# Products with V over 128 + 128 + 80 keys per 64 queries, in a windowed attention and convolution block

## The chip, the cores and the metric

The kernel runs on one core of a Trainium2 chip. The metric is device time in microseconds, from runs of the whole program; the profile is one execution, recorded by the hardware profiler. Short names: PE is TensorE's matmul stream and PEld its weight loads, DVE is VectorE, ACT ScalarE, POOL GpSimd, SP SyncE, which here only issues DMAs.

## What is computed

One encoder layer over two sequences (256 and 2048 tokens, so 2 + 16 blocks of 128) with 16 learned meta tokens ahead of each: RMSNorm, one input projection, a windowed attention group beside a convolution group, gates, one output projection, and the residual. What matters here is the attention of a real query t: it sees all 16 meta keys and the real keys s with |t - s| <= 128, in 8 heads of 64 with 2 key/value heads.

```python
kw = concatenate([kp[:, :-2], kp[:, 1:-1], kp[:, 2:]], axis=2)   # left, own and right block
vw = concatenate([vp[:, :-2], vp[:, 1:-1], vp[:, 2:]], axis=2)
s_win = einsum('bnqkgd,bnskd->bnkgqs', qb, kw) * scale - slopes * dist   # -inf outside the window
s_meta = einsum('bnqkgd,bmkd->bnkgqm', qb, km) * scale
p = softmax(concatenate([sink_b, s_meta, s_win], axis=-1), axis=-1)
o = einsum('bnkgqm,bmkd->bnqkgd', p[..., 1:17], vm) + einsum('bnkgqs,bnskd->bnqkgd', p[..., 17:], vw)
```

Outside the sequence there are no keys: blocks 0 and 2 have no left neighbour, blocks 1 and 17 no right one. These four are called edge blocks here, the other fourteen full blocks.

## The kernel before

Matrix operands are kept as a high and a low part in a 32-bit format (float32r), so that a product takes two or three matmuls. The first two thirds of the time are the input projection (`proj_et`, `proj_te`, lines 830 to 861) with the convolution on DVE; then come attention and the output projection.

Attention goes by steps of eight slots (`slot_step`, line 599). Step s computes the scores of block s and, for block s - 1, the products with V; the output projection (`outproj`, line 575) gives two pieces of three 512-column matmuls to every slot. The first 14 slots run between projection groups (`spread`, line 632), the rest in `attention_rest` (line 653). In that last stretch the order of the work on PE and on POOL is the program's own (`MAN2`); the orders of DVE, ACT and SP come from a planner's simulated times. `tick` ends a slot, and `later(k, f)` puts f off by k ticks.

- **Scores** (`scores`, line 376): each slot takes 32 queries of the 4 heads of one key/value head, as 128 rows, in two matmuls into one PSUM bank. A full block's window is `SW` = 304 keys wide (128 + 16 meta + 128 + 32). DVE adds the position bias and takes the minimum (`bias_max`, line 403), ACT does the exponential (`expo`), and after the fourth slot of a head group `norm` (line 427) divides on POOL; it first writes the 16 meta columns out to a tile `pm` (line 430).
- **Transposes** (`bank`, line 455): `plan` (line 448) lists them: for each key/value head and each tile of 128 keys (left, own, right) four 128x128 transposes of the probabilities, which load the probabilities as weights and stream the identity. Between the two heads stands one meta bank of two transposes, of `pm`. ACT copies the high part, DVE subtracts for the low part (`split`, line 464).
- **Products** (`pv_mm`, line 492): two matmuls of 512 columns for each tile of keys and head, high and low part. The meta product (`pv_meta`, line 499) is one further matmul of 512 columns for each head; its operand is spread over the heads by two masked products on POOL (`spread_meta`, line 480), and its weights `vm` hold the meta V eight times (eight DMAs, line 1135).
- **Loads** (on SP): `load_k` (line 281) issues one or two DMAs for a block into one of two key tiles, at slot 0 of the step before its use; `load_v` (line 289) one DMA of 128 KB for a block, in five buffers.

`merge` (line 517) adds the halves of the product and gates it on POOL with `gat`, which `load_ga` loads at slot 1.

Of the kernel before, what the change touches and what calls it, by code (L numbers as in the profile page):

```python
# [18 lines left out]
P = 128  # L19
# [60 lines left out]
def hymba_kernel(  # L80
# [29 lines left out]
    vec = const.tile([P, 30], F32, name="vec")  # L110
# [4 lines left out]
    snk, msk, nsnk = vec[:, 22:24], vec[:, 24:28], vec[:, 28:30]  # L115
    vm = const.tile([P, KV, P], F32R, name="vm")
# [114 lines left out]
    vt, qt, q2t, sbt, pmt, gat, gct, cnt, mix, att, yot, opj = ({} for _ in range(12))  # L231
# [3 lines left out]
    def attention_open():  # L235

        phase[0] = 2
        right_pools.close()
        man = ExitStack()
        cst['man'] = man  # L240
        man.enter_context(tc.manual_schedule(engines=MAN1))
        ap = att_pools.enter_context(tc.tile_pool(name="ap", bufs=2, side="right", reuse_waits="tile"))
        pool["a"] = ap
        cst["bias"] = bias = ap.tile([P, KV, 4, SW], BF16, tag="bias", name="bias", bufs=1)
        load_q(0)
        for i in range(2):
            kw.append(ap.tile([P, 2, KV, 400], F32R, tag=f"kw{i}", name=f"kw{i}", bufs=1))
        load_k(0)
        nc.sync.dma_start(bias, bias_c)
        for t in kw:  # L250
            nc.gpsimd.tensor_copy(t[:, :, :, P : P + NM], km)
        for i in range(3):
            t = ap.tile([P, 4, 400], F32, tag=f"sb{i}", name=f"sb{i}", bufs=1)
            for n in range(4):
                if n > 0:
                    nc.vector.memset(t[:, n, 0 : QB * n], 0.0)
                if n < 3:
                    nc.vector.memset(t[:, n, QB * n + SW : 400], 0.0)
            sbs.append(t)
        load_v(0)  # L260
        load_v(1)
# [17 lines left out]
    vt, qt, q2t, sbt, pmt, gat, gct, cnt, mix, att, yot, opj = ({} for _ in range(12))  # L279

    def load_k(b):
        if has_left(b):
            nc.sync.dma_start(kw[b % 2][:, :, :, 0:P].bitcast(F32), kd[:, :, :, P * (b - 1) : P * b])
        hi = P * (b + 2) if has_right(b) else P * (b + 1)
        nc.sync.dma_start(
            kw[b % 2][:, :, :, P + NM : P + NM + hi - P * b].bitcast(F32), kd[:, :, :, P * b : hi]
        )
# [88 lines left out]
    def scores(b, kv, n):  # L376

        c0 = QB * n if has_left(b) else P
        c1 = QB * n + SW if has_right(b) else min(QB * n + SW, 400 - P)
        w = c1 - c0  # L380
        if n == 0:
            sbt[b, kv] = sbs[(2 * b + kv) % 3]
            stat[b, kv] = (
                pool["a"].tile([P, 4], F32, tag="nm", name=f"nm{b}_{kv}", bufs=3),
                pool["a"].tile([P, 4], F32, tag="rs", name=f"rs{b}_{kv}", bufs=3),
                pool["a"].tile([P, 4], F32, tag="es", name=f"es{b}_{kv}", bufs=3),
            )
            if kv == 0:
                pmt[b] = pool["a"].tile([P, KV, 2, 4, NM], F32, tag="pm", name=f"pm{b}", bufs=1)
# [37 lines left out]
        def norm():  # L427
            nc.vector.tensor_tensor(es, es, rs, op=ALU.add)
            nc.vector.reciprocal(es, es)
            nc.gpsimd.tensor_tensor(  # L430
                pmt[b][:, kv],
                sb[:, :, P : P + NM].unsqueeze(1).to_broadcast([P, 2, 4, NM]),
                es.unsqueeze(1).unsqueeze(3).to_broadcast([P, 2, 4, NM]),
                op=ALU.mult,
            )
            for k in range(4):
                a0 = QB * k if has_left(b) else P
                a1 = QB * k + SW if has_right(b) else min(QB * k + SW, 400 - P)
# [9 lines left out]
    def plan(b):  # L448
        ks = ([0] if has_left(b) else []) + [1] + ([2] if has_right(b) else [])
        return [(k, 0) for k in ks] + [("m", 0)] + [(k, 1) for k in ks]  # L450

    KCOL = (0, P + NM, 2 * P + NM)
    pv_st = {}

    def bank(b, k, kv):
        pt = psum.tile([P, 4, P], F32, tag="b", name=f"pT{b}_{k}_{kv}")
        if k == "m":
            for i in range(KV):
                nc.tensor.transpose(pt[:, i, :], pmt[b][:, i].rearrange("p a h m -> p (a h m)"), ident)  # L459
        else:  # L460
            for hl in range(4):
                nc.tensor.transpose(pt[:, hl, :], sbt[b, kv][:, hl, KCOL[k] : KCOL[k] + P], ident)  # L462

        def split():
            if k == "m":
                ph = pool["a"].tile([P, KV, P], F32R, tag="phm", name=f"phm{b}", bufs=1)
                nc.scalar.copy(ph, pt[:, 0:KV, :])
                nc.vector.tensor_tensor(ph[64:128], pt[64:128, 0:KV, :], ph[64:128], op=ALU.subtract)
                later(1, lambda: spread_meta(b, ph))
                return  # L470
            ph, pl = (pt_part(2 * (n_bank[0] % 3) + i) for i in range(2))
            n_bank[0] += 1
            nc.scalar.copy(ph, pt)  # L473
            nc.vector.tensor_tensor(pl, pt, ph, op=ALU.subtract)  # L474
            pv_st[b, k, kv] = (ph, pl)

        later(1, split)
        later(3 if k == "m" else 2, lambda: pv(b, k, kv))

    def spread_meta(b, ph):  # L480

        pd = cst["pt"][:, 6:8].rearrange("p a (j n) -> p a j n", n=P)
        for kv in range(KV):
            nc.gpsimd.tensor_tensor(
                pd[:, kv],
                ph[:, kv : kv + 1, :].to_broadcast([P, 4, P]),
                msk.unsqueeze(2).to_broadcast([P, 4, P]),
                op=ALU.mult,
            )
        pv_st[b, "m"] = pd  # L490

    def pv_mm(b, kv, lhs, hs, start, stop):
        if start:
            opj[b, kv] = psum.tile([P, 4, P], F32, tag="c", name=f"O{b}_{kv}")
        o = opj[b, kv]
        for i, t in enumerate(hs):
            nc.tensor.matmul(o, lhs, t, start=(start and i == 0), stop=(stop and i == 1))  # L497

    def pv_meta(b, kv, stop):
        pin(stop)(nc.tensor.matmul)(  # L500
            opj[b, kv], vm[:, kv, :], pv_st[b, "m"][:, kv], start=False, stop=stop
        )

    def pv(b, k, kv):
        if k == "m":
            pv_meta(b, 0, True)
            later(1, lambda: merge(b, 0))
            return
        ks = [x for x, y in plan(b) if y == kv and x != "m"]
        first, last = k == ks[0], kv == 1 and k == ks[-1]  # L510
        pv_mm(b, kv, vt[b - 1 + k][:, kv, :], pv_st[b, k, kv], first, last)
        if kv == 1 and first:
            pv_meta(b, 1, False)
        if last:
            later(1, lambda: merge(b, 1))
# [83 lines left out]
    def slot_step(s_, slot):  # L599
        a, bb = s_, s_ - 1  # L600
        has_a, has_b = a < NB, 0 <= bb < NB
        steps = plan(bb) if has_b else []
        if slot == 0:
# [11 lines left out]
        if slot < len(steps):  # L615
# [59 lines left out]
    if True:  # L675
# [424 lines left out]
        nc.sync.dma_start(vec[:, 0:28], vecs)  # L1100
# [130 lines left out]
def layout(inputs):  # L1231
# [58 lines left out]
```

## Time and profile before

| | |
|---|---|
| time, median of 3 runs | 955.31 us (954.71 to 955.47) |
| span of the profiled execution | 953.4 us |
| instructions | 16429 |
| matmuls and transposes on PE | 5813 |
| busy share PE / PEld / DVE / ACT / POOL | 99% / 94% / 79% / 45% / 35% |
| moved by DMA | 170.88 MB, mean 179 GB/s |

For the profiled execution only its span is given, from the first to the last instruction; the time of a run also holds what lies around it. A busy PE is not PE at its peak: the ends of matmuls are modelled and overlap the next one's start, so distances between starts, and the pieces of the chain of waits, are the measure of what an instruction costs.

### The profile page before, as it was taken

What the parts mean: (1) busy time and instruction counts of PE and PEld (TensorE: products, weight loads), DVE (VectorE), ACT (ScalarE), POOL (GpSimd) and SP (SyncE); (2) the same over time, 40 slices, a digit from 0 to 9 for tenths busy, and PEclk for the clock granted to TensorE, in tenths of its full rate; (3) what the DMA queues carried; (4) which work ended last, traced back from release to release, by engine and by line L of the source; (5) the groups of instructions that cost most, each with busy time, mean ns of one, the idle gap of its engine ahead of it and who ended that gap; (6) DMA issues with size and microseconds to landing.
All of it is one profiled execution on the core that took longest, in us unless ns stands there. A gap on an engine that the chain in (4) does not pass through costs nothing.

```text
span 953.4 us, 16429 instructions
## 1 busy us (share of the span) xinstructions
PE 948.1 (99%) x5813; PEld 893.4 (94%) x5813; DVE 756.9 (79%) x1282; ACT 427.4 (45%) x1170; POOL 336.6 (35%) x518
## 2 busy tenths in 40 slices
PE   9999999999999999999999999999999999999998
PEld 8999999999999999999999999988888888888887
DVE  5579999997977879999995666677776777767773
ACT  7432022353458750011112446666665666656661
POOL 3320000282488300000001446556454544545442
PEclk9999999999999999999999999999999999999999
DMA  8575345785656594233333587945554455544311
GB/s 296 174 262 202 133 174 182 252 294 175 185 179 193 194 319 145 89 113 138 131 138 133 175 289 271 383 148 179 169 167 128 144 162 163 167 129 142 130 56 67
DMA packets 121585, 170.88 MB, mean 179 GB/s; under 512 B 9984, under 2 KB 84112, under 8 KB 121504
## 3 DMA queue, kind: packets, MB, share of 16 engines
q1 hardware_dynamic: 121504, 169.84, 53.3%
q8 instruction: 46, 0.75, 0.3%
q14 instruction: 35, 0.29, 0.1%
HBM read 107.10 MB, written 62.70 MB: 178 GB/s over the span
## 4 chain that ended last, share of the span: by engine, by line
PE 92%; DVE 3%; DMA 3%; SPq 1%; issue 1%; POOL 0%; ACT 0%; DVEq 0%; POOLq 0%; ACTq 0%
PE pj L837 42%; PE y L583 20%; PE pj L853 12%; PE O L497 5%; PE pT L462 4%; PE S L349 4%; PE O L349 1%; DVE y L920 1%; PE lnu L220 1%; PE lnt L201 1%; PE qT L349 1%; DMA wraw<-in_w_in 1%; DMA kd<-ks 1%; DMA vmd<-vs-1_2072 1%; PE pT_m L459 0%
## 5 line engine op out<-in xcount | busy, mean ns | idle before, releaser
L837 PE MATMUL pj<-xh,ws 128*128 128x384 f32 (+1 forms) x1536 | 395.9, 338 | 0.1
L920 DVE SCALAR_TENSOR_TENSOR y<-us,cw,y 128x1167 f32<-128x1167 f32 x240 | 328.7, 1422 | 0.4
L837 PEld LDWEIGHTS pj<-xh,ws 128*128 128x128 f32 x1536 | 280.0, 188 | 0.4 <-ACT xh L1090 0.4
L837 PE MATMUL pj<-xl,ws 128*128 128x384 f32 (+1 forms) x768 | 260.9, 340 | 0.1
L583 PE MATMUL y<-wo,rest 128*128 128x512 f32 (+1 forms) x672 | 173.7, 396 | 0.0
L853 PE MATMUL pj<-ws,xh 128*128 128x256 f32 (+1 forms) x880 | 165.6, 284 | 0.4 <-DVE qs L984 0.3
L837 PEld LDWEIGHTS pj<-xl,ws 128*128 128x128 f32 x768 | 144.1, 188 | 0.5 <-DVE xl L775 0.4
L853 PEld LDWEIGHTS pj<-ws,xh 128*128 128x128 f32 (+1 forms) x880 | 136.4, 187 | 1.4 <-issue 0.5
L583 PEld LDWEIGHTS y<-wo,rest 128*128 128x128 f32 x672 | 116.5, 189 | 19.6
L853 PE MATMUL pj<-ws,xl 128*128 128x256 f32 (+1 forms) x440 | 123.9, 282 | 0.0
L416 ACT ACTIVATE sb<-sb,nm 128x304 f32<-128x304 f32 (+4 forms) x144 | 77.1, 536 | 64.8 <-DVE nm L404 62.7
L945 ACT ACTIVATE go<-pj 128x384 f32<-128x384 f32 x48 | 23.6, 491 | 155.7 <-PE pj L837 141.6
L474 DVE TENSOR_TENSOR ptiles<-pT,ptiles 128x512 fp32r<-128x512 f32 x100 | 68.5, 685 | 30.6 <-ACT ptiles L473 29.8
L404 DVE CUSTOM_DVE_ANT_0 sb<-S,bias,vec 128x304 f32<-128x304 f32 (+4 forms) x144 | 73.6, 511 | 17.0 <-PE S L349 14.4
L128 POOL TENSOR_SCALAR ssk<-ssk 128x2 f32<-128x2 f32 x18 | 7.5, 419 | 213.4 <-ACT sqk L959 211.4
L853 PEld LDWEIGHTS pj<-ws,xl 128*128 128x128 f32 (+1 forms) x440 | 82.2, 187 | 0.3
L439 POOL TENSOR_SCALAR sb<-sb,es 128x304 f32<-128x304 f32 (+4 forms) x144 | 72.3, 519 | 3.5
L473 ACT CAST ptiles<-pT 128x512 fp32r<-128x512 f32 x100 | 58.0, 580 | 32.3 <-PE pT L462 31.5
L497 PE MATMUL O<-ptiles,v 128*128 128x512 f32 x200 | 64.8, 402 | 0.0
L349 PEld LDWEIGHTS S<-kw,q 128*128 128x128 f32 x288 | 53.2, 188 | 11.0
L349 PE MATMUL S<-kw,q 128*128 128x304 f32 (+4 forms) x288 | 62.1, 297 | 0.0
L128 POOL TENSOR_SCALAR ssq<-ssq 128x4 f32<-128x4 f32 (+2 forms) x55 | 30.3, 550 | 87.4 <-ACT xn L700 69.7
(127 smaller groups left out, 1277.0 us busy)
## 6 DMA issues: line engine op xcount, KB each, us to landing
wd<-ws SPq DMA_DIRECT2D x36, 512.0 KB, 6.0
ws<-wd SPq DMA_DIRECT2D x36, 512.0 KB, 5.9
wraw<-in_w_in SPq DMA_DIRECT2D x52, 256.0 KB, 6.0
xn<-in_z SPq DMA_DIRECT2D x18, 512.0 KB, 5.3
gd<-go SPq DMA_DIRECT2D x48, 192.0 KB, 2.0
yo<-in_z SPq DMA_DIRECT2D x36, 256.0 KB, 3.3
out_y<-yo SPq DMA_DIRECT2D x35, 256.0 KB, 2.2
kw<-kd SPq DMA_DIRECT2D x16, 512.0 KB, 5.0
```

Of the source, the lines that this page charges most:

```text
L349: r = f(*a, **k)
L404: nc.vector.tensor_tensor_reduce(out=sb[:, n, c0:c1], in0=ps[:, 0:w], in1=cst["bias"][:, kv, n, c0 - QB * n : c1 - QB * n], scale=1.0, sca ...
L416: nc.scalar.activation(sb[:, n, c0:c1], sb[:, n, c0:c1], AF.Exp, bias=nm[:, n : n + 1], scale=-1.0, accum_out=rs[:, n : n + 1],)
L439: nc.gpsimd.tensor_scalar(sb[:, k, a0:a1], sb[:, k, a0:a1], es[:, k : k + 1], 1.0, op0=ALU.mult, op1=ALU.mult)
L462: nc.tensor.transpose(pt[:, hl, :], sbt[b, kv][:, hl, KCOL[k] : KCOL[k] + P], ident)
L473: nc.scalar.copy(ph, pt)
L474: nc.vector.tensor_tensor(pl, pt, ph, op=ALU.subtract)
L497: nc.tensor.matmul(o, lhs, t, start=(start and i == 0), stop=(stop and i == 1))
L583: nc.tensor.matmul(ps, mh[mi][:, e % 4, :], wo[e, wi][:, cols], start=(e == 4 and k == 0), stop=(e == 3 and k == 2),)
L837: nc.tensor.matmul(ps[:, :n], ws[:, d, wi, P * half_i : P * half_i + P], x[xi][:, d, o : o + n], start=(k == 0), stop=(k == 3 * ND - 1),)
L853: nc.tensor.matmul(ps[:rows, :UW], x[xi][:, d, o : o + rows], ws[:, d, wi, :], start=(k == 0), stop=(k == 3 * ND - 1),)
L920: nc.vector.scalar_tensor_tensor(y[:, yo + o0 : yo + o1], u[:, o0 + k : o1 + k], cw[:, j, k : k + 1], y[:, yo + o0 : yo + o1], op0=ALU.mul ...
```

## The change

For 64 queries (two of the 32-query groups) the window is 64 + 256 = 320 keys, and 336 with the meta keys. The keys are laid out anew in the key tile, so that these 336 come in three transposes: `c`, the own block's 128 keys; `m`, the nearer halves of the left and the right block; `x`, 80 rows, the 16 meta keys with the far half of the left block (for the first 64 queries) or of the right one (for the last 64). The meta bank, its product, its POOL work and `vm` go. `c` and `m` take two products of 512 columns, `x` four of 256. The fourth score group is 336 keys wide in place of 304. At edge blocks `m` has 64 keys and one half of `x` only the 16 meta keys, but the three banks stay; the 64 missing keys that lie inside a span get scores too, which DVE overwrites. K comes in five DMAs (rows of 256 bytes but for the first, 512), V in seven, each block's V being read up to three times; `load_v` moves from two steps ahead to slot 3 of the block's score step.

```diff
+LA, MA, CC, LB, RA, MB, RB, KW = 0, 64, 80, 208, 272, 336, 352, 416
+SPANS = ((LA, RA + QB), (LA + QB, MB), (CC, RB + QB), (CC, KW))
+XR = QC + NM
-    vm = const.tile([P, KV, P], F32R, name="vm")
...
-        for t in kw:
-            nc.gpsimd.tensor_copy(t[:, :, :, P : P + NM], km)
+        for t, c0 in zip(kw, (LB, RA)):
+            for at in (MA, MB):
+                nc.gpsimd.tensor_copy(t[:, :, :, at : at + NM], km)
+            nc.gpsimd.memset(t[:, :, :, c0 : c0 + QC].bitcast(F32), 0.0)
...
     def load_k(b):
+        t = kw[b % 2].bitcast(F32)
+        at = P * (b - 1)
+        nc.sync.dma_start(t[:, :, :, CC:LB], kd[:, :, :, at + P : at + 2 * P])
         if has_left(b):
-            nc.sync.dma_start(kw[b % 2][:, :, :, 0:P].bitcast(F32), kd[:, :, :, P * (b - 1) : P * b])
...
+            nc.sync.dma_start(t[:, :, :, LA:MA], kd[:, :, :, at : at + QC])
+            nc.sync.dma_start(t[:, :, :, LB:RA], kd[:, :, :, at + QC : at + P])
+        if has_right(b):
+            nc.sync.dma_start(t[:, :, :, RA:MB], kd[:, :, :, at + 2 * P : at + 2 * P + QC])
+            nc.sync.dma_start(t[:, :, :, RB:KW], kd[:, :, :, at + 2 * P + QC : at + 3 * P])
 
     def load_v(b):
-        vt[b] = pool["a"].tile([P, KV, P], F32R, tag="v", name=f"v{b}", bufs=5)
-        nc.sync.dma_start(vt[b].rearrange("p a e -> p (a e)").bitcast(F32), vd[b])
+        vt[b] = [
+            pool["a"].tile([P, KV, P], F32R, tag=f"v{k}", name=f"v{k}_{b}", bufs=VBUFS) for k in ("c", "m", "a", "b")
+        ]
+        c, m, a, z_ = (t.rearrange("p a e -> p (a e)").bitcast(F32) for t in vt[b])
+        nc.sync.dma_start(c, vd[b])
...
+            nc.sync.dma_start(m[0:QC], vd[b - 1, QC:P])
+            nc.sync.dma_start(a[0:QC], vd[b - 1, 0:QC])
+        nc.sync.dma_start(a[r : r + NM], vmd)
+        nc.sync.dma_start(z_[0:NM], vmd)
+        if has_right(b):
+            nc.sync.dma_start(m[r : r + QC], vd[b + 1, 0:QC])
+            nc.sync.dma_start(z_[NM:XR], vd[b + 1, QC:P])
+
+    def span(b, n):
+        c0, c1 = SPANS[n]
+        if not has_left(b):
+            c0 = max(c0, MA)
+        if not has_right(b):
+            c1 = min(c1, RA if n < 2 else RB)
+        return c0, c1
...
         def bias_max():
+            off = masked(b, n)
+            if off is not None:
+                nc.vector.memset(ps[:, off - c0 : off - c0 + QC], BIG)
...
         def norm():
...
-            nc.gpsimd.tensor_tensor(
-                pmt[b][:, kv],
...
+    PLAN = [("c", 0), ("m", 0), ("x", 0), None, ("c", 1), ("m", 1), ("x", 1)]
...
     def bank(b, k, kv):
         pt = psum.tile([P, 4, P], F32, tag="b", name=f"pT{b}_{k}_{kv}")
+        sb = sbt[b, kv]
+        rows = [P] * 4
+        for n in range(4):
+            if k == "c":
+                src = sb[:, n, CC:LB]
+            elif k == "m":
+                src = sb[:, n, LB if has_left(b) else RA : MB if has_right(b) else RA]
+                rows[n] = src.shape[-1]
+            else:
+                r = rows[n] = edges(b)[n // 2]
+                src = sb[:, n, MB : MB + r] if n >= 2 else sb[:, n, CC - r : CC]
+            nc.tensor.transpose(pt[: rows[n], n, :], src, ident)
...
-    def spread_meta(b, ph):
...
+    def pv(b, k, kv):
+        parts = pv_st[b, k, kv]
+        tc_, tm, ta, tb = vt[b]
...
+        if k != "x":
+            r = P if k == "c" or (has_left(b) and has_right(b)) else QC
+            for i, t in enumerate(parts):
+                nc.tensor.matmul(
+                    o, (tc_ if k == "c" else tm)[:r, kv, :], t[:r], start=(k == "c" and i == 0), stop=False
+                )
             return
...
+        for h, (t, r) in enumerate(zip((ta, tb), edges(b))):
+            for i, p in enumerate(parts):
+                nc.tensor.matmul(
+                    o[:, 2 * h : 2 * h + 2],
+                    t[:r, kv, :],
+                    p[:r, 2 * h : 2 * h + 2],
+                    start=False,
+                    stop=(h == 1 and i == 1),
+                )
+        later(1, lambda: merge(b, kv))
...
         if slot == 0:
             if a + 1 < NB:
                 load_q(a + 1)
                 load_k(a + 1)
-            if a + 2 < NB:
-                load_v(a + 2)
...
+        if slot == VSLOT and 0 < a < NB:
+            load_v(a)
...
-                for r0 in range(0, P, NM):
-                    nc.sync.dma_start(vm[r0 : r0 + NM].rearrange("p a e -> p (a e)").bitcast(F32), vmd)
...
-    nc = bacc.Bacc("TRN2", target_bir_lowering=False, num_devices=1)
+    nc = bacc.Bacc("TRN2", target_bir_lowering=False, num_devices=1, dynamic_dma_scratch_size=1024)
```

The rest of the diff renames columns of the constants, builds the bias table for the new order of keys, and lets `split` rotate through four pairs of buffers where it had three.

## Rows read from the trace of the kernel before

**Rows 1.** Page, parts 1 and 2: busy time, and the granted clock in 40 slices.

```profile
PE 948.1 (99%) x5813; PEld 893.4 (94%) x5813; DVE 756.9 (79%) x1282; ACT 427.4 (45%) x1170; POOL 336.6 (35%) x518
PEclk9999999999999999999999999999999999999999
```

**Rows 2.** Page, part 4: the chain that ended last, shares by engine.

```profile
PE 92%; DVE 3%; DMA 3%; SPq 1%; issue 1%; POOL 0%; ACT 0%; DVEq 0%; POOLq 0%; ACTq 0%
```

**Rows 3.** Windows: one step; PE, PEld, DVE, ACT, POOL busy, clock, DMA share, GB/s.

```profile
763.54:783.42 19.88, 19.88 (x110) 16.93 (x109) 14.79 (x39) 12.41 (x33) 9.71 (x15) 1.00 0.48 150
```

**Rows 4.** Chain of waits, pieces of one step: start us, us until the next piece.

```profile
657.83 0.28 PE S L349 x2
658.11 0.46 PE O L497 x2
658.57 0.44 PE pT L462 x4
...
662.78 0.23 PE O L349
```

**Rows 5.** Chain of waits, projection: matmuls of 256 columns.

```profile
289.18 5.68 PE pj L853 x48
```

**Rows 6.** Groups of PE by form, whole span: products with V and transposes.

```profile
L497 PE MATMUL O<-ptiles,v 128*128 128x512 f32 x200 | 64.8, 402 | 0.0
L462 PE MATMUL pT<-ident,sb 128*128 128x128 f32 x400 | 60.0, 272 | 0.0
```

**Rows 7.** Groups of PEld by form: weight loads of 128 and of 16 columns.

```profile
L853 PEld LDWEIGHTS pj<-ws,xh 128*128 128x128 f32 x864 | 134.9, 188 | 1.1 <-issue 0.5 <-DVE qs L984 0.4
L853 PEld LDWEIGHTS pj<-ws,xh 128*16 128x16 f32 x16 | 1.5, 94 | 0.3
```

**Rows 8.** Timeline of PE at the start: transposes that stream 16 and 128 columns.

```profile
5.91 0.82 PE L1082 MATMUL xt<-ident,xn 16*128 16x16 f32 x6
6.66 2.50 PE L1075 MATMUL warmup<-ident 128*128 128x128 f32 x10
...
10.79 0.82 PE L1082 MATMUL xt<-ident,xn 128*128 128x128 f32 x6
11.45 0.83 PE L1075 MATMUL warmup<-ident 128*128 128x128 f32 x6
```

**Rows 9.** Timeline of PE: the meta transposes of three steps, and what follows.

```profile
617.13 0.64 PE L459 MATMUL pT_m<-ident,pm 128*128 128x128 f32 x2
617.52 1.63 PE L583 MATMUL y<-wo,rest 128*128 128x512 f32 x6
...
635.16 0.69 PE L459 MATMUL pT_m<-ident,pm 128*128 128x128 f32 x2
635.61 1.63 PE L583 MATMUL y<-wo,rest 128*128 128x512 f32 x6
...
656.06 0.38 PE L459 MATMUL pT_m<-ident,pm 128*128 128x128 f32 x2
656.19 1.64 PE L583 MATMUL y<-wo,rest 128*128 128x512 f32 x6
```

**Rows 10.** DMA: issues to landing; SP's timeline in one step; packets from 764 to 804.

```profile
kw<-kd SPq DMA_DIRECT2D x16, 512.0 KB, 5.0
...
768.39 0.62 SPq L285 DMA_DIRECT2D kw<-kd  x1
...
771.06 0.38 SPq L330 DMA_DIRECT2D ga<-gd  x1
780.65 0.34 SPq L595 DMA_DIRECT2D out_y<-yo  x1
...
q1 hardware_dynamic: 6238, 6.03, 47.9%
```

**Rows 11.** Timelines of POOL and PE: the second head's division, and its first transposes.

```profile
772.23 2.14 POOL L439 TENSOR_SCALAR sb<-sb,es 128x304 f32<-128x304 f32 x4
...
777.69 0.60 PE L462 MATMUL pT<-ident,sb 128*128 128x128 f32 x4
```

More of the change, by code (lines that the diff above doesn't have):

```diff
@@ L55 @@
 MSLOT = 0
+VSLOT = 3
+VBUFS = 2
 QB = 32
 SW = 2 * P + NM + QB
+QC = P // 2
+LA, MA, CC, LB, RA, MB, RB, KW = 0, 64, 80, 208, 272, 336, 352, 416
+SPANS = ((LA, RA + QB), (LA + QB, MB), (CC, RB + QB), (CC, KW))
+BOFF = (0, SW, 2 * SW, 3 * SW, 4 * SW + QB)
+XR = QC + NM
 PIN_X = 7
@@ L109, in hymba_kernel @@
     make_identity(nc, ident)
-    vec = const.tile([P, 30], F32, name="vec")
+    vec = const.tile([P, 26], F32, name="vec")
     nw = vec[:, 0:8]
@@ L114, in hymba_kernel @@
     lb = vec[:, 16:20]
[L115 to L116 removed]
+    snk, nsnk = vec[:, 22:24], vec[:, 24:26]
     km = const.tile([P, 2, KV, NM], F32R, name="km")
@@ L230, in hymba_kernel @@
     pool, cst, kw, wo, wo_slot, sbs = {}, {}, [], {}, {}, []
-    vt, qt, q2t, sbt, pmt, gat, gct, cnt, mix, att, yot, opj = ({} for _ in range(12))
+    vt, qt, q2t, sbt, gat, gct, cnt, mix, att, yot, opj = ({} for _ in range(11))
     OUT_ORDER = (4, 5, 6, 7, 0, 1, 2, 3)
@@ L243, in attention_open @@
         pool["a"] = ap
-        cst["bias"] = bias = ap.tile([P, KV, 4, SW], BF16, tag="bias", name="bias", bufs=1)
+        cst["bias"] = bias = ap.tile([P, KV, BOFF[4]], BF16, tag="bias", name="bias", bufs=1)
         load_q(0)
         for i in range(2):
-            kw.append(ap.tile([P, 2, KV, 400], F32R, tag=f"kw{i}", name=f"kw{i}", bufs=1))
+            kw.append(ap.tile([P, 2, KV, KW], F32R, tag=f"kw{i}", name=f"kw{i}", bufs=1))
         load_k(0)
         nc.sync.dma_start(bias, bias_c)
-        for t in kw:
-            nc.gpsimd.tensor_copy(t[:, :, :, P : P + NM], km)
+        for t, c0 in zip(kw, (LB, RA)):
+            for at in (MA, MB):
+                nc.gpsimd.tensor_copy(t[:, :, :, at : at + NM], km)
+            nc.gpsimd.memset(t[:, :, :, c0 : c0 + QC].bitcast(F32), 0.0)
         for i in range(3):
[L253 to L258, printed above, removed]
+            t = ap.tile([P, 4, KW], F32, tag=f"sb{i}", name=f"sb{i}", bufs=1)
+            for n, c0 in enumerate((RA + QB, LA, RB + QB)):
+                nc.vector.memset(t[:, n, c0 : c0 + QB], 0.0)
             sbs.append(t)
         load_v(0)
-        load_v(1)
     def mixing_open():
@@ L277, in has_right, with masked @@
         return b not in (NB_P - 1, NB - 1)
-    vt, qt, q2t, sbt, pmt, gat, gct, cnt, mix, att, yot, opj = ({} for _ in range(12))
+    vt, qt, q2t, sbt, gat, gct, cnt, mix, att, yot, opj = ({} for _ in range(11))
     def load_k(b):
+        t = kw[b % 2].bitcast(F32)
+        at = P * (b - 1)
+        nc.sync.dma_start(t[:, :, :, CC:LB], kd[:, :, :, at + P : at + 2 * P])
         if has_left(b):
-            nc.sync.dma_start(kw[b % 2][:, :, :, 0:P].bitcast(F32), kd[:, :, :, P * (b - 1) : P * b])
[L284 to L287, printed above, removed]
-    def load_v(b):
-        vt[b] = pool["a"].tile([P, KV, P], F32R, tag="v", name=f"v{b}", bufs=5)
-        nc.sync.dma_start(vt[b].rearrange("p a e -> p (a e)").bitcast(F32), vd[b])
+            nc.sync.dma_start(t[:, :, :, LA:MA], kd[:, :, :, at : at + QC])
[3 more added lines that the diff above has]
+            nc.sync.dma_start(t[:, :, :, RB:KW], kd[:, :, :, at + 2 * P + QC : at + 3 * P])
+    def load_v(b):
+        vt[b] = [
[3 more added lines that the diff above has]
+        nc.sync.dma_start(c, vd[b])
+        r = QC if has_left(b) else 0
+        if has_left(b):
+            nc.sync.dma_start(m[0:QC], vd[b - 1, QC:P])
[12 more added lines that the diff above has]
+        return c0, c1
+    def masked(b, n):
+        if not has_left(b):
+            return LB
+        if n >= 2 and not has_right(b):
+            return RA
+        return None
     def load_q(b):
@@ L376, in scores @@
     def scores(b, kv, n):
-        c0 = QB * n if has_left(b) else P
-        c1 = QB * n + SW if has_right(b) else min(QB * n + SW, 400 - P)
+        c0, c1 = span(b, n)
         w = c1 - c0
@@ L429, in norm @@
             nc.vector.reciprocal(es, es)
-            nc.gpsimd.tensor_tensor(
-                pmt[b][:, kv],
[L432 to L435, printed above, removed]
             for k in range(4):
-                a0 = QB * k if has_left(b) else P
-                a1 = QB * k + SW if has_right(b) else min(QB * k + SW, 400 - P)
+                a0, a1 = span(b, k)
                 nc.gpsimd.tensor_scalar(
@@ L446, in scores, with edges @@
             later(3, norm)
[L448 to L452, printed above, removed]
+    PLAN = [("c", 0), ("m", 0), ("x", 0), None, ("c", 1), ("m", 1), ("x", 1)]
     pv_st = {}
+    def edges(b):
+        return (XR if has_left(b) else NM, XR if has_right(b) else NM)
     def bank(b, k, kv):
         pt = psum.tile([P, 4, P], F32, tag="b", name=f"pT{b}_{k}_{kv}")
[L457 to L462, printed above, removed]
-        def split():
[L465 to L471, printed above, removed]
@@ L472, in split @@
+        def split():
+            ph, pl = (pt_part(2 * (n_bank[0] % 4) + i) for i in range(2))
             n_bank[0] += 1
-            nc.scalar.copy(ph, pt)
-            nc.vector.tensor_tensor(pl, pt, ph, op=ALU.subtract)
+            halves = ((0, 4, rows[0]),) if rows[0] == rows[3] else ((0, 2, rows[0]), (2, 4, rows[3]))
+            for n0, n1, r in halves:
+                nc.scalar.copy(ph[:r, n0:n1], pt[:r, n0:n1])
+                nc.vector.tensor_tensor(pl[:r, n0:n1], pt[:r, n0:n1], ph[:r, n0:n1], op=ALU.subtract)
@@ L475, in split @@
             pv_st[b, k, kv] = (ph, pl)
         later(1, split)
-        later(3 if k == "m" else 2, lambda: pv(b, k, kv))
-    def spread_meta(b, ph):
[L482 to L490, printed above, removed]
@@ L492, in pv_mm @@
-    def pv_mm(b, kv, lhs, hs, start, stop):
-        if start:
+        later(2, lambda: pv(b, k, kv))
+    def pv(b, k, kv):
+        parts = pv_st[b, k, kv]
+        tc_, tm, ta, tb = vt[b]
+        if k == "c":
             opj[b, kv] = psum.tile([P, 4, P], F32, tag="c", name=f"O{b}_{kv}")
         o = opj[b, kv]
[L496 to L507, printed above, removed]
-            return
[L509 to L515, printed above, removed]
+        if k != "x":
[4 more added lines that the diff above has]
+                )
+            return
@@ L601, in slot_step @@
         has_a, has_b = a < NB, 0 <= bb < NB
-        steps = plan(bb) if has_b else []
+        steps = PLAN if has_b else []
         if slot == 0:
@@ L614, in slot_step @@
             load_x(bb)
-        if slot < len(steps):
+        if slot < len(steps) and steps[slot]:
             bank(bb, *steps[slot])
@@ L1099, in hymba_kernel @@
         r = {0: stats(0)}
-        nc.sync.dma_start(vec[:, 0:28], vecs)
+        nc.sync.dma_start(vec[:, 0:24], vecs)
         for i in (1, 2, 3):
@@ L1258, in layout @@
     slopes = np.exp2(-8.0 * np.arange(1, H + 1, dtype=np.float32) / H).astype(np.float32)
-    bias_c = np.zeros((P, KV, 4, SW), np.float32)
+    bias_c = np.zeros((P, KV, BOFF[4]), np.float32)
     for kv in range(KV):
         for n in range(4):
-            col = QB * n + np.arange(SW)
-            key = np.where(col < P, col - P, col - P - NM)
+            col = np.arange(*SPANS[n])
+            seg = np.searchsorted([MA, CC, LB, RA, MB, RB], col, side="right")
+            key = col - np.array([P, 0, CC, RA, RA - P, 0, RA - P + NM])[seg]
+            meta = (seg == 1) | (seg == 5)
             dist = np.abs(key[None, :] - (QB * n + row % QB)[:, None]).astype(np.float32)
             full = np.where(dist <= P, slopes[4 * kv + local][:, None] * dist, np.float32(BIG))
-            bias_c[:, kv, n] = np.where(((col >= P) & (col < P + NM))[None, :], np.float32(0.0), full)
-    mask = ((np.arange(P)[:, None] // NM) % 4 == np.arange(4)[None, :]).astype(np.float32)
+            bias_c[:, kv, BOFF[n] : BOFF[n + 1]] = np.where(meta[None, :], np.float32(0.0), full)
     w_out = f["w_out"][0].reshape(8, P, D)
-    vecs = np.concatenate([vecs, sink, mask], axis=1)
+    vecs = np.concatenate([vecs, sink], axis=1)
     bias_c = bias_c.astype(ml_dtypes.bfloat16)
```

4 lines of the change are left out of this document (1 added, 3 removed).

## Prediction

> **What bounds the kernel now.** First the page's busy shares and the clock: PE is busy 948.1 of 953.4 us, at the full granted clock (2.4 GHz) in all 40 slices [rows 1]. So no clock is to be won or lost as long as PE stays fed. A busy PE could still hide waits, so next the chain that ended last: 92% of it is PE [rows 2]. Then the stretch that the change is in, the steady attention steps, by windows: one step takes 19.88 us, all of it PE, while DVE is busy 14.79, ACT 12.41 and POOL 9.71 us [rows 3]. The last view is the chain's pieces inside a step: one group of matmuls hands over to the next with nothing between them, so a piece's length is what its instructions cost PE: 0.28 us for two score matmuls of 304 columns, 0.46 for two products of 512, 0.23 for the single meta product, 0.44 for four transposes [rows 4]. What the change takes from PE comes off the time, what it adds goes on; work on DVE, ACT, POOL and the queues counts only where PE begins to wait for it.
>
> **Prices.** A product of 512 columns is 0.23 us, a transpose 0.11 [rows 4]. A matmul of 256 columns is 5.68 / 48 = 0.118 us [rows 5]. A score column costs 1 / 2.4 GHz = 0.417 ns at the granted clock [rows 1]; 304 of them make 0.127 of the 0.14 us of a score matmul, the rest being fixed.
>
> The price that the trace does not show is a transpose of 80, 64 or 16 keys. It loads fewer weight columns and streams the same 128 columns of the identity (0.053 us). What bounds a transpose today? Not the stream: at the start six transposes that stream 16 columns take 6.66 - 5.91 = 0.75 us, six that stream 128 take 11.45 - 10.79 = 0.66 [rows 8], no less for an eighth of the columns. A weight load does depend on its columns: 188 ns for 128, 94 ns for 16 [rows 7], so 94 / 112 = 0.84 ns a column, and 128 x 0.84 = 107 ns is just the 0.11 us of a transpose. I take it that transposes are bound by their loads. Then 80 columns save 48 x 0.84 = 40 ns (0.07 us left), 64 save 54 ns and end about at the streaming floor (0.056), and 16 end there too. The bounds: no gain, 0.11 for each; and all at the floor of 0.053.
>
> **A full block's step** (14 of 18 blocks).
> - Products with V: before 3 tiles x 2 heads x 2 parts + 2 meta = 14 of 512 columns; after, 8 of 512 and 8 of 256. 6 x 0.23 leave, 8 x 0.118 come: -0.436 us.
> - Transposes: before 24 + 2 meta, after 24: -0.22. Of the 24, eight have 80 columns: -8 x 0.040 = -0.32.
> - Scores: the fourth group grows from 304 to 336 columns, in 4 matmuls: +128 columns, +0.053.
>
> Sum -0.92 us a step, times 14: -12.9 us.
>
> **An edge block's step** (blocks 0, 1, 2 and 17). Before, two tiles in place of three: 8 + 2 products, 16 + 2 transposes. This can be checked against the page: 14 x 24 + 4 x 16 = 400 transposes and 14 x 12 + 4 x 8 = 200 products [rows 6]. After, three banks as everywhere.
> - Products: 10 x 0.23 = 2.30 becomes 8 x 0.23 + 8 x 0.118 = 2.78: +0.48.
> - Transposes: 18 x 0.11 = 1.98 becomes 8 x 0.11 + 8 x 0.056 (64 keys) + 4 x 0.07 + 4 x 0.056 (16 keys) = 1.83: -0.15.
> - Scores: without a left block the widths go from 176, 208, 240, 272 to 240, 272, 304, 336; times 4 matmuls +1024 columns, +0.43 us. Without a right one 272, 240, 208, 176 become 272, 240, 272, 272: +640 columns, +0.27.
>
> That is +0.76 and +0.60, two blocks of each: +2.7 us. The window drawn tighter pays only where there are three blocks of keys.
>
> **Two stalls go.** The meta transposes wait for POOL's `pm` in the first steps: from their start to the next matmul 0.39 and 0.45 us where 0.13 is usual, 0.26 + 0.32 = 0.6 us [rows 9]. `pm` no longer exists; what is late next is the division of the second head, which loses `pm` ahead of it on POOL and today ends at 772.23 + 2.14 = 774.4, 3.3 us before its first transposes [rows 11].
>
> **Costed at nothing, and the cover.** ACT and DVE lose the meta split, POOL the meta column copy and the two spreads; the fourth group is a tenth wider on all three. Even at its 14.8 us of now [rows 3] DVE, the nearest of them, fits a 19 us step with 4 us left: PE covers them. DVE's memset at edge blocks stands ahead of `bias_max` in DVE's own order, in four or eight places a block; the PSUM bank that it holds longer is wanted two slots later. The first head's merge moves two slots forward and POOL's gate with it, ahead of `norm` in POOL's written order: `gat` is issued in slot 1 and would be wanted in slot 5, some 9 us on. SP loses the eight `vm` issues, which lay beside the projection; PE's whole idle time in the span is 953.4 - 948.1 = 5.3 us [rows 1], so little can come of that. It gets nine more issues a step: three more for K (0.62 us each at most) and six more for V (0.38, as `ga`), some 4.1 us. SP stands idle from 771.44 to 780.65 in each step [rows 10], and the V loads of slot 3 fall into that gap. They wait for the buffers of the block two before, whose last product runs in slot 0. K is issued a whole step before its use and lands 5.0 us after issue now [rows 10]; V's lead shrinks to seven slots, 17 us. The smaller DMA scratch I cost at nothing: all but a few packets of that stretch are on SP's hardware queue [rows 10].
>
> **Sum.** -12.9 + 2.7 - 0.6 = -10.8 us, from 953.4 to 942.6 us of span. The profiled execution has no time of its own besides its span; the median of the runs, 955.31, is 1.9 us above it, for what lies around, and I keep that: 944.5 us.
>
> **Rivals.**
> 1. *Narrow transposes are no cheaper* (a fixed cost bounds them). Then a full step saves 0.436 + 0.22 - 0.053 = 0.60, in all 8.4; an edge step has +0.48 + 6 x 0.11 and its scores, 1.57 or 1.41, in all +6.0; with the stalls -3.0 us: 952.3 us. For it: no transpose narrower than 128 keys is in the trace, and six of 16 streamed columns were even slower than of 128. Against it: the fit of 107 ns with 0.11.
> 2. *Narrow transposes are dearer.* If a load of 128 columns runs in a faster mode than narrower ones, at twice the speed a column, 80 columns cost 2 x 80 x 0.84 = 134 ns: +0.024 each in place of -0.040. A full step then saves 0.60 - 0.19 = 0.41, in all 5.7. At an edge 64 columns cost 107 ns, as 128 do now, and 16 the floor: 16 x 0.11 + 4 x 0.056 + 4 x 0.134 = 2.52, +0.54, so the step loses 1.45 or 1.29, in all 5.5. With the stalls -0.8: 954.5 us, no change. The row speaks against it, as 16 columns took half of 128 [rows 7]. The Trainium skill has such a rule ("TensorE: Matmul & The Clock Gate", section on weight-path perf modes): fast weight load needs all 128 columns, and it leaves out fp32. By its second half these fp32 transposes never had the mode, and no run here shows either half.
> 3. *Slower: the DMA engines become the bound.* Place: the first score matmul of each step, which needs all of K. K's pieces turn from 1024 packets a block into 2560, most of 256 bytes, V's from 128 into 416: 1824 more a step. In the 40 us window 6238 packets took 47.9% of 16 engines, 0.479 x 16 x 40 / 6238 = 49 ns each [rows 10]. At that price they add 5.7 us to the 9.5 us that the engines are busy in a step (0.48 of 19.88) [rows 3], still under 19. If price went by bytes, 0.29 MB at 150 GB/s would be 2 us. The point from which it decides is (19 - 9.5) x 16 / 1824 = 83 ns a packet. At 100 ns the engines would need 9.5 + 11.4 = 20.9 us a step, +1.9 over the new 19.0, in 14 steps +27: some 971 us. The Trainium skill ("DMA: Bandwidth & Descriptors", Specifications) does ask for 512 bytes and more for full rate and speaks of read-modify-write below; no run here shows rows of 256 bytes.
>
> That the change does not do what it says can be left out: the counts follow from the code.
>
> **How the numbers follow.** Forecast with cheaper narrow transposes 0.68; rival 1, 0.17; rival 2, 0.05; rival 3 or a smaller version of it 0.06; another small loss that ends within 0.2% 0.04. A measurement of this kernel can tell about 0.2%, 1.9 us. The first two are faster by more than that, except some of rival 1's spread: faster 0.84, same 0.09, slower 0.07. The low end takes all narrow transposes at the streaming floor (8 x 0.017 x 14 = 1.9) and 256 columns at 107 ns (144 x 0.011 = 1.6): 944.5 - 3.5 = 941.0. The high end takes in rival 1: 953.0.
>
> **What would show it.** In the profile after: PE's transposes 432 in place of 436 (400 + 36), 144 products each of 512 and of 256 columns; a full step of about 18.95 us by windows, still all PE; a bank of 80 rows at 0.28 us in the chain, not 0.44; weight loads of 80 columns some 40 ns under those of 128. Steps of 19.3 us with banks at 0.44 are rival 1. PE idle at a step's first score, with K's landing far over 5 us and the DMA share near 1, is rival 3. A PE gap released by POOL at slot 4 or 0 would mean that the order on POOL was tighter than read here.

## The result, and the profile after

The changed kernel takes 957.33 us (median of 11 runs, 957.21 to 958.21). The kernel before, on the same chip and beside it, takes 954.75 (11 runs, 954.50 to 955.73). The ratio is 1.0026 (95% interval 1.0017 to 1.0035): 2.6 us slower. The forecast was 944.5 us in a range of 941.0 to 953.0, so the time lies outside it, and on the other side of no change.

First the page of the kernel after: busy time, granted clock, and the chain's shares by engine (parts 1, 2 and 4).

```profile
PE 949.3 (99%) x5861; PEld 893.3 (93%) x5861; DVE 757.8 (79%) x1295; ACT 429.0 (45%) x1168; POOL 286.8 (30%) x450
...
PEclk9999999999999999999999999999999999999999
...
PE 95%; DVE 2%; DMA 1%; issue 1%; POOL 0%; ACT 0%; SPq 0%; DVEq 0%; ACTq 0%
```

Beside [rows 1, 2]: PE has 48 more instructions (5861 for 5813), POOL has lost 50 us of work, and the clock is full in every slice. The chain is still PE. Nothing has taken PE's place, so the extra time has to be in what PE's own instructions cost. Next one full step by windows (PE, PEld, DVE, ACT, POOL busy, clock, DMA share, GB/s), the counterpart of [rows 3].

```profile
769.55:788.81 19.26, 19.26 (x110) 16.70 (x109) 14.37 (x38) 12.12 (x32) 6.94 (x11) 1.00 0.61 175
```

It takes 19.26 us for 19.88: a full step did become faster, by 0.62 us, though not by the 0.92 of the forecast. Fourteen of them give 8.7 us. A kernel that wins 8.7 us in its full blocks and ends 2.6 later has lost some 11 elsewhere. Now the chain of waits in that step (start us, us until the next piece), beside [rows 4].

```profile
772.15 0.48 PE O L523 x4
772.63 0.44 PE pT_c L494 x4
...
774.74 0.44 PE pT_m L494 x4
...
777.30 0.44 PE pT_x L494 x4
```

All three banks take 0.44 us, `pT_x` of 80 keys as well, where 0.28 was forecast. Four products of 256 columns and 80 rows take 0.48 us, 0.12 each as priced. So the full step is rival 1's: 0.60 by its sum, 0.62 measured. The weight loads by form (busy us, mean ns of one | idle time before, and what ended it) show that the narrow loads did get shorter:

```profile
L494 PEld LDWEIGHTS pT_c<-ident,sb 128*128 128x128 f32 x144 | 16.6, 141 | 0.4
L494 PEld LDWEIGHTS pT_x<-ident,sb 128*80 128x80 f32 x128 | 14.5, 118 | 5.0
L494 PEld LDWEIGHTS pT_x<-ident,sb 128*16 128x16 f32 x16 | 1.3, 89 | 0.9 <-issue 0.2
```

141, 118 and 89 ns for 128, 80 and 16 columns: the loads followed the columns, and the bank did not follow the loads.

The rest is in the edge blocks. The chain at the products of a block without a left neighbour:

```profile
640.50 0.46 PE O L517 x2
640.95 0.44 PE pT_x L494 x4
641.39 1.39 PE y L598 x6
642.78 0.28 PE S L383 x2
643.06 0.66 PE O L517 x2
643.72 1.58 PE y L598 x6
...
645.61 0.86 PE O L523 x4
646.48 0.44 PE pT_c L494 x4
```

The two products at 643.06 take 0.66 us, the two at 640.50 take 0.46, and the six projection matmuls behind the first pair 1.58 for the 1.39 before them. The four products of 256 columns take 0.86 for 0.48. The timelines of PE and of PEld (start us, us busy, count; in brackets the idle time before and what ended it) tell these products apart by their rows, the number ahead of the `*`.

```profile
640.33 0.62 PE L517 MATMUL O<-ptiles,vc 128*128 128x512 f32 x2
...
642.99 0.73 PE L517 MATMUL O<-ptiles,vm 64*128 64x512 f32 x2
643.65 1.65 PE L598 MATMUL y<-wo,rest 128*128 128x512 f32 x6
...
645.54 0.50 PE L523 MATMUL O<-ptiles,va 16*128 16x256 f32 x2
```

```profile
640.19 0.33 PEld L517 LDWEIGHTS O<-ptiles,vc 128*128 128x128 f32 x2
...
642.99 0.29 PEld L517 LDWEIGHTS O<-ptiles,vm 64*128 64x128 f32 x2 [0.18 <-ACT ptiles L501]
643.65 1.22 PEld L598 LDWEIGHTS y<-wo,rest 128*128 128x128 f32 x6 [0.37 <-issue]
...
645.54 0.29 PEld L523 LDWEIGHTS O<-ptiles,va 16*128 16x128 f32 x2 [0.21 <-issue]
...
771.84 0.34 PEld L523 LDWEIGHTS O<-ptiles,va 80*128 80x128 f32 x2
```

The pair at 640.33 has 128 rows, and its first weight load begins at 640.19, under the matmul before it. The pair at 642.99 has 64 rows, and its load begins at 642.99 too: it was not pulled ahead. Nor was the load of the 128-row matmul behind it (643.65 on both engines, after 0.37 us without a load), nor that of the 16-row pair (645.54 on both). A switch between 128 rows and 64 or fewer lays the load open, twice for each pair. At 80 rows it does not happen: the load at 771.84, in a full block, begins 0.15 us ahead of its matmul (771.99). The bracket at 642.99 names a copy by ACT into another bank, `x`, which is no operand of this pair; such an opening stands before the other narrow pairs too, behind changing names.

Rival 3's place shows no wait: PE waits 1.3 us for `ident` and 1.0 for the first `xn` at the start, 0.2 in the projection, and no wait of PE is put down to a DMA. The DMA queue from 764 to 804 (packets, MB, share of 16 engines), beside [rows 10]:

```profile
q1 hardware_dynamic: 10176, 6.62, 57.8%
```

0.578 x 16 x 40 / 10176 = 36 ns a packet, under the 49 of before. Both are means over packets of all sizes. By size, the trace has 18 ns for each of the 4096 packets of 256 bytes in this window and 28 for those of 512. The engines are busy 0.61 x 19.26 = 11.7 us a step.

### The profile page after: what moved, and what is told of

Its sections match the earlier page's. It is cut to its first block, busy times and chain, and to the rows that moved or that the text cites. A ratio compares the mean times of both kernels' runs of the same rounds, so it can differ in the third digit from the quotient of the medians.

```text
span 955.9 us, 16841 instructions
## 1 busy us (share of the span) xinstructions
PE 949.3 (99%) x5861; PEld 893.3 (93%) x5861; DVE 757.8 (79%) x1295; ACT 429.0 (45%) x1168; POOL 286.8 (30%) x450
## 4 chain that ended last, share of the span: by engine, by line
PE 95%; DVE 2%; DMA 1%; issue 1%; POOL 0%; ACT 0%; SPq 0%; DVEq 0%; ACTq 0%
PE pj L852 42%; PE y L598 21%; PE pj L868 14%; PE S L383 4%; PE O L517 4%; PE O L523 2%; PE pT_c L494 2%; PE pT_x L494 2%; PE pT_m L494 2%; PE qT L383 1%; PE lnt L207 1%; PE lnu L226 1%; DVE y L935 1%; DMA kd<-ks 1%; DMA xn<-in_z 0%
## 5 line engine op out<-in xcount | busy, mean ns | idle before, releaser
L450 ACT ACTIVATE sb<-sb,nm 128x304 f32<-128x304 f32 (+3 forms) x144 | 79.2, 550 | 48.2 <-DVE nm L438 47.6
L438 DVE CUSTOM_DVE_ANT_0 sb<-S,bias,vec 128x304 f32<-128x304 f32 (+3 forms) x144 | 76.2, 529 | 28.9 <-PE S L383 26.1
L550 POOL TENSOR_TENSOR at<-at,ga 128x256 f32<-128x256 f32 x36 | 26.4, 735 | 201.8 <-DVE at L544 130.8
L466 POOL TENSOR_SCALAR sb<-sb,es 128x304 f32<-128x304 f32 (+3 forms) x144 | 75.9, 544 | 26.5 <-DVE es L463 20.6
L383 PE MATMUL S<-kw,q 128*128 128x304 f32 (+3 forms) x288 | 64.1, 304 | 0.0
L134 POOL TENSOR_SCALAR ssq<-ssq 128x4 f32<-128x4 f32 (+2 forms) x55 | 26.7, 485 | 92.8 <-ACT xn L715 74.1
L895 ACT ACTIVATE sg<-pj 128x384 f32<-128x384 f32 (+1 forms) x24 | 11.8, 493 | 82.6 <-PE pj L852 73.8
L598 PE MATMUL y<-wo,mch 128*128 128x512 f32 x144 | 47.3, 410 | 0.0
```

Of the source, the lines that this page charges most:

```text
L134: nc.gpsimd.tensor_scalar(src, src, scale, eps, op0=ALU.mult, op1=ALU.add)
L383: r = f(*a, **k)
L438: nc.vector.tensor_tensor_reduce(out=sb[:, n, c0:c1], in0=ps[:, 0:w], in1=cst["bias"][:, kv, BOFF[n] + c0 - SPANS[n][0] : BOFF[n] + c1 - S ...
L450: nc.scalar.activation(sb[:, n, c0:c1], sb[:, n, c0:c1], AF.Exp, bias=nm[:, n : n + 1], scale=-1.0, accum_out=rs[:, n : n + 1],)
L466: nc.gpsimd.tensor_scalar(sb[:, k, a0:a1], sb[:, k, a0:a1], es[:, k : k + 1], 1.0, op0=ALU.mult, op1=ALU.mult)
L550: nc.gpsimd.tensor_tensor(at[:, pr, :], at[:, pr, :], gat[b][:, pr, :], op=ALU.mult)
```

## The experiments

Two theories stood after the result. **R**: products of 64 or 16 rows among 128-row ones cost PE 0.37 to 0.39 us a pair more, and there are 16 such pairs (4 edge blocks, 2 heads, one 64-row pair in `m` and one 16-row pair in `x`). **D**, the rival: the products only wait at the edge blocks, for the planner's order or for data, and their rows don't matter. For the transposes, **S**: a 32-bit transpose is bound by the columns of the identity that it streams.

**e1, `m` at 128 rows.** At edge blocks the missing 64 keys get V rows of the block itself and probabilities of zero.

```diff
-            nc.sync.dma_start(m[0:QC], vd[b - 1, QC:P])
-            nc.sync.dma_start(m[r : r + QC], vd[b + 1, 0:QC])
+        nc.sync.dma_start(m[0:QC], vd[b - 1 if has_left(b) else b, QC:P])
+        nc.sync.dma_start(m[QC:P], vd[b + 1 if has_right(b) else b, 0:QC])
...
+            if not has_right(b) and n < 2:
+                nc.vector.memset(sb[:, n, RA:MB], 0.0)
...
-            r = P if k == "c" or (has_left(b) and has_right(b)) else QC
+            r = P
```

> Only the m products of the four edge blocks change: 128 rows in place of 64 (the 64 missing keys have probability zero). Theory R (few rows): a pair of products with 64 or fewer rows among 128-row ones costs about 0.37 us more, because its weight load and the next one are not overlapped; 8 such pairs, so -3.0 us, about 954.4, and in the edge steps the pair takes 0.46 us and not 0.66. Rival D (late operands): the edge products wait for ACT and DVE, which have memsets and a split in two parts there; m is split in one part before and after, so no change, 957.3.

Measured 953.75 us (10 runs), 0.9988 (0.9979 to 0.9997) of the kernel before (954.71, 27 runs, which serve e1 to e4), 3.6 us under the change. More rows and more bytes, and a shorter time: for `m`, D falls.

**e2, both halves of `x` at 80 rows**, by the same means.

```diff
-        return (XR if has_left(b) else NM, XR if has_right(b) else NM)
+        return (XR, XR)
```

> Only the x products of the four edge blocks change: 80 rows for both halves, in place of 16 and 80; the split of that bank becomes one part. Theory R: 8 pairs of 16 rows go, -2.9 us, about 954.4. Rival D: up to the whole unexplained 5.8 us, about 951.5, as the split in two parts is gone.

Measured 956.66 us (10 runs), 1.0019 (1.0010 to 1.0029): only 0.7 us better than the change. Its timeline of PE:

```profile
609.29 0.47 PE L385 MATMUL S<-kw,q 128*128 128x240 f32 x2
610.16 0.49 PE L523 MATMUL O<-ptiles,vc 128*128 128x512 f32 x1 [0.40 <-ACT ptiles L507]
...
611.58 0.49 PE L523 MATMUL O<-ptiles,vc 128*128 128x512 f32 x1 [0.92 <-DVE ptiles L508]
612.00 0.50 PE L523 MATMUL O<-ptiles,vm 64*128 64x512 f32 x1
...
617.18 0.40 PE L529 MATMUL O<-ptiles,va 80*128 80x256 f32 x2
617.41 0.40 PE L529 MATMUL O<-ptiles,vb 80*128 80x256 f32 x2
```

The products of `x` now follow each other in 0.23 us, so the padding did what R says. But where the planner's order goes over into the written one, ACT and DVE deliver the split of a bank late, and PE waits 0.40 + 0.92 = 1.3 us in a place where it did not wait before. The same place in the change:

```profile
609.06 0.47 PE L383 MATMUL S<-kw,q 128*128 128x240 f32 x2
...
609.83 0.60 PE L494 MATMUL pT_x<-ident,sb 128*16 128x128 f32 x4
```

Idle time understates the loss, as the modelled ends of the matmuls cover part of it. By starts, from these score matmuls to what follows the two products of `vc`, it is 612.00 - 609.29 = 2.71 us in e2 and 609.83 - 609.06 = 0.77 in the change: 1.9 us lost. The expected 2.9 less 1.9 makes 1.0, and 0.7 was measured. One pair of 64 rows also stands apart in e2, with a single product at 612.00. In the planner's order of e2 the last two of the four transposes that feed `vc` run at 608.47; in the change all four ran at 605.06.

**e3, both.**

> Both of the former. Theory R: the two gains add, -5.9 us, about 951.4, faster than the kernel before by some 3 us. Rival D: no more than with x alone.

Measured 952.99 us (11 runs), 0.9982 (0.9974 to 0.9991): 4.3 us under the change, faster than the kernel before, and 1.6 above what was expected. The same stall, 1.9 us by starts, makes up for that. The chain in the block shown above:

```profile
642.09 0.28 PE S L385 x2
642.37 0.47 PE O L525 x2
...
644.53 0.48 PE O L531 x4
645.01 0.44 PE pT_c L502 x4
```

From the score matmuls to `pT_c` it takes 645.01 - 642.09 = 2.92 us, and 646.48 - 642.78 = 3.70 in the change: 0.78 for one pair of 64 rows and one of 16, 0.39 each. The transposes of `x` take 0.44 in both, with 80 keys in all four here and 16 in two of the four there.

**e4, 64 rows in full blocks.** If rows decide, a product that is cut from 80 rows to 64 must become dearer.

```diff
         for h, (t, r) in enumerate(zip((ta, tb), edges(b))):
+            r = min(r, QC) if has_left(b) and has_right(b) else r
```

> The dose raised: in the 14 full blocks the x products take 64 of their 80 rows, so the meta keys of the first 64 queries and 16 far keys of the last 64 are left out. Transposes, splits and loads stay. Theory R: 28 groups of four products now have 64 rows, each group +0.37 us or more, so a step of 19.26 becomes about 20.0 us and the time about 968. Rival D, and any reckoning by the amount of work: no change, 957.3, as fewer rows cannot take longer.

Measured 967.32 us (one run), 10.0 above the change. Its chain:

```profile
753.59 0.44 PE qT L383 x4
...
756.20 0.66 PE O L524 x4
756.86 0.58 PE pT_c L494 x4
...
773.51 0.44 PE qT L383 x4
```

A step takes 773.51 - 753.59 = 19.92 us, 0.66 more than the change's 19.26. Four products take 0.66 in place of 0.48, and the transposes behind them 0.58 in place of 0.44: 0.32 a head. Fewer rows, and 10 us more. It is the sharpest of the runs for R: nothing waits here for new data, nor does the order change. Its timelines of PEld and of PE also say what it is about rows that costs:

```profile
756.12 0.29 PEld L524 LDWEIGHTS O<-ptiles,va 64*128 64x128 f32 x2 [0.21 <-ACT sb L450]
756.35 0.30 PEld L524 LDWEIGHTS O<-ptiles,vb 64*128 64x128 f32 x2
756.79 0.42 PEld L494 LDWEIGHTS pT_c<-ident,sb 128*128 128x128 f32 x4
...
756.47 0.39 PE L524 MATMUL O<-ptiles,vb 64*128 64x256 f32 x2
```

Between one 64-row product and the next the load does run ahead: that of `vb` begins at 756.35, its matmul at 756.47. Only the first load going in (756.12) and the first coming out (756.79) begin with their own matmuls. So it is the change of rows that PE pays for, at both ends of a run of narrow products, and not each narrow product.

**e5, a version without the narrow products.** At an edge block the 16 meta keys move into the free half of `m`, POOL copies their probabilities there, and that half of `x` has no transposes and no products at all; the rows of `m` left over get probabilities of zero. All products then have 128 or 80 rows.

```diff
+                if k < 2 and not has_left(b):
+                    nc.gpsimd.tensor_copy(sb[:, k, LB : LB + NM], sb[:, k, MA : MA + NM])
+                if k >= 2 and not has_right(b):
+                    nc.gpsimd.tensor_copy(sb[:, k, RA : RA + NM], sb[:, k, MB : MB + NM])
...
+    def halves(b):
+        return [h for h in range(2) if (has_left(b), has_right(b))[h]]
...
-        for h, (t, r) in enumerate(zip((ta, tb), edges(b))):
+        r, hs = XR, halves(b)
+        for h in hs:
```

> On top of the padded rows of both kinds, the edge blocks' 16 meta probabilities of the half without a neighbour are copied by POOL into the masked keys of m, with the meta V in the same rows, so that half of x falls away there: two transposes and two products of 256 columns for each of 8 heads. If PE's stream sets the time: 8 x (2 x 0.11 + 2 x 0.118) = 3.6 us under the padded kernel's 952.99, about 949.4. Rival: the small POOL copies stand in the written order ahead of the transposes and make PE wait; then 953 or more.

Measured 947.41 us (5 runs) beside 954.60 of the kernel before (9 runs): 0.9926 (0.9912 to 0.9940). It beats both kernels, by 7.2 and 9.9 us. From the change's 957.33 go 16 x 0.39 = 6.2 us for the narrow pairs, and at each of 4 blocks 4 transposes of 0.11 and 4 products of 0.118, 3.6 us: 947.5. It is 2.0 under the 949.4 expected, which started from e3 and its stall. The stall does not come up here: PE waits for no split of a bank, and the four transposes that feed `vc` run at 603.08. The chain at an edge block:

```profile
617.30 0.22 PE pT_x L499 x2
...
621.34 0.24 PE O L527 x2
```

Two transposes for 0.22, two products for 0.24, at the prices of a full block.

**e6, transposes that stream 96 columns.** They take 96 of 128 partitions of the probabilities and 96 columns of the identity; the keys, and so the loads, are as in the change.

```diff
-            nc.tensor.transpose(pt[: rows[n], n, :], src, ident)
+            nc.tensor.transpose(pt[: rows[n], n, 0:96], src[0:96], ident[0:96, 0:96])
```

> What bounds a transpose: all transposes of the probabilities read 96 of 128 rows and stream 96 columns of the identity, weight loads keep their columns. The fourth head of each group is left out of the products' operand (zeros). Theory S (a 32-bit transpose streams its columns at half speed, 128 x 2 / 2.4 GHz = 107 ns): a transpose falls from 0.11 to 0.083 us, a bank of four from 0.44 to 0.33, a step of 19.26 to about 18.6. Theory L (loads) or F (a fixed cost): 0.44 and 19.26 stay.

Measured 949.08 us (one run). A chain and a group of PEld:

```profile
765.27 0.44 PE qT L384 x4
...
768.35 0.33 PE pT_c L495 x4
...
772.87 0.33 PE pT_x L495 x4
...
784.05 0.44 PE qT L384 x4
```

```profile
L495 PEld LDWEIGHTS pT_c<-ident,sb 96*128 96x128 f32 x144 | 14.8, 140 | 0.4
```

With loads of an unchanged 140 ns all three banks (`pT_m` as well) fall from 0.44 to 0.33 us, as 96 to 128. The step takes 784.05 - 765.27 = 18.78 us, 0.48 less than the change; six banks at 0.11 would be 0.66, but the projection behind a bank now takes 1.41 or 1.42 for 1.38 or 1.39. That is 0.44 / 4 / 128 = 0.33 / 4 / 96 = 0.86 ns a streamed column, about two cycles of the full clock. The run cuts the partitions that are read together with the columns, so by itself it does not tell the two apart. For products the partitions do not set the time: with 64 rows (e4, within the run) and with 80 they follow each other in the same 0.12 us.

## Why the prediction was wrong

**What held.** PE stays the bound, at full clock, as read from [rows 1 to 3]; DVE, ACT and POOL stay covered (14.37, 12.12 and 6.94 us of 19.26). The products of 256 columns cost 0.12 us with 80 rows. The meta stalls are gone: the `m` bank of four takes 0.44 and the projection follows. The nine more DMA issues a step, the seven slots of lead for V and the smaller packets cost PE nothing. Rival 3 failed on its price: it needed 83 ns a packet, and the mean was 36, with 18 for the 256-byte rows. (Its 5.7 us should read 5.6; and the trace of before does hold packets of 256 bytes, 128 of them, at 18 ns.)

**First step that failed: "I take it that transposes are bound by their loads."** They are bound by the stream of the identity, at half the rate that I gave it: 128 columns are 0.11 us and not 0.053 (e6). So no narrow transpose came cheaper, rival 1 was right about this term, and 7.8 us were lost against the forecast, 4.5 in full blocks and 3.3 at edges. The fit of 107 ns was a coincidence: 128 columns at two cycles come to 107 ns as well, and 0.84 ns a column was read from the projection's loads, where those of the transposes go from 89 ns at 16 columns to 141 at 128, 0.46 a column.

What had excluded the stream were the six 16-column transposes of [rows 8], and that row was misread. They ran at the lower level of TensorE's clock, and were set beside 128-column ones at the full clock. The first fence has what stands between the two in the kernel before, the second the same six in the changed kernel (timelines of PE):

```profile
8.96 1.49 PE L1082 MATMUL xt<-ident,xn 128*128 128x128 f32 x6
10.24 0.72 PE L1075 MATMUL warmup<-ident 128*128 128x128 f32 x4
```

```profile
5.70 0.54 PE L1097 MATMUL xt<-ident,xn 16*128 16x16 f32 x6
6.17 1.38 PE L1090 MATMUL warmup<-ident 128*128 128x128 f32 x10
```

Six transposes of 128 columns take 10.24 - 8.96 = 1.28 us there, and 0.66 from 10.79 on. In between, with PE at work since 1.34 us, the distances halve, as from 1.2 to 2.4 GHz: this trace's record of the granted clock begins with the full level at 10.45 us, and the views count what lies ahead of the record as full, so that [rows 1] reads 9 in every slice. At one and the same clock it is 0.75 for 16 columns and 1.28 for 128. In the changed kernel the record begins at 4.98 us, and the same six take 6.17 - 5.70 = 0.47 us, against 0.66. So fewer streamed columns were cheaper, with loads of 128 columns each: the row spoke for the stream.

Rival 2 failed as well, as narrower loads were shorter and the banks stayed at 0.44. The Trainium skill ("TensorE: Matmul & The Clock Gate", Weight-path perf modes) asks for all 128 columns for fast weight load, and leaves out fp32; the runs agree with its second half, as loads of 80 columns took 118 ns for 141.

**Second step that failed: the price of the edge blocks' products, "8 x 0.23 + 8 x 0.118".** It counts columns alone. The step reckoned with the 64 and 16 keys of the transposes, but not with their return as rows of the products. The change of rows cost 0.39 us more for each of the 16 narrow pairs, 6.2 in all, as e1 to e5 show. With rival 1's +6.0 for the edge blocks, they lose 12.2 us, where I had 2.7 and rival 1 6.0. No rival held this; those on the slower side looked to DMA and to loads, and the range ended at rival 1.

**The sum, made anew.** -8.7 for the full steps, +6.0 for the edges by rival 1, +6.2 for narrow pairs, -0.6 for the stalls as forecast: +2.9 us. The medians give +2.6. From the start of the same piece of the projection to the end, the change takes 955.9 - 512.84 = 443.06 us and the kernel before 953.4 - 513.40 = 440.0, +3.06; what lies ahead of that piece differs between the two profiles by half a us.

**On rows.** The Trainium skill ("TensorE: Matmul & The Clock Gate", Why this matters for your kernels) says that a single matmul of 32 rows takes as long as one of 128. No run here has one by itself. Within a run of narrow products e4 agrees, at 64 rows: 0.12 us, as with 80. For a pair among 128-row matmuls it does not carry over: 16 and 64 rows cost 0.39 us more, 80 rows nothing.

**How the runs add up, and what stays open.** By the distances between starts in the timeline of the change, the eight 64-row pairs cost 3.4 us (in block 0 the two products of one pair stand apart, and each pays by itself) and the eight 16-row pairs 2.9. That makes 3.4 for e1 (3.6 measured), 2.9 - 1.9 = 1.0 for e2 (0.7, with one more pair apart), 6.3 - 1.9 = 4.4 for e3 (4.3), and with the 3.6 of its transposes and products 9.9 for e5 (9.9). Why the planner puts two transposes later in e2 and e3 was not tried, nor rows between 64 and 80, nor what in PE makes a change of rows cost this.

## What to carry to other kernels

Where PE sets the time, price a matmul by its columns and by whether its rows change from its neighbours': cutting a product to 64 rows or fewer among full ones can cost more than it saves, and padding with zeros (e3) or folding the few keys into a tile that is there anyway (e5) is cheaper. Do the sum for the edge blocks with the same care as for the steady ones; here 4 blocks of 18 undid what 14 had won. Before a row serves to exclude a cause, look at everything in it that differs from the case at hand; here it was the clock, which the distances between equal instructions showed and the view of it did not.

## What the runs showed of the hardware

- Among 128-row matmuls, weight loads for 128 and 80 rows begin under the matmul before; the first load for 64 or 16 rows, and the next one for 128, begin only with their own matmul. It cost 0.39 us for a pair and 0.32 for four products of 256 columns; between 64-row products loads run ahead (e4).
- A 32-bit transpose costs 0.86 ns a streamed column (0.11 us for 128, 0.083 for 96), whether its load takes 141 ns, 118 or 89.
- DMA packets took 18 ns for 256 bytes and 28 for 512. The mean over all sizes came down from 49 to 36 ns as 256-byte rows became many: 63% more packets for 10% more bytes, with 21% more engine time.
- The first ten microseconds of PE ran at half the clock in the trace of before (0.21 us a transpose against 0.11), and the first five in that of the change.
